# Rotating 96 images: all stores moved from SyncE to GpSimd, each transfer asked for as one packet per engine

## The chip, the cores and the metric

The kernel runs on one core of one Trainium2 chip. The metric is the device time of that core in microseconds (us); lower is better. One execution was also taken by the hardware profiler, and all views below are of that one.

## The reference

The input is 32 x 3 = 96 images of 256 x 256 float32 values. Each is turned by 90 degrees clockwise.

```python
def reference(x: np.ndarray) -> np.ndarray:
    return np.rot90(x, k=-1, axes=(-2, -1)).astype(np.float32)
```

There is no arithmetic in it. 25.17 MB are read from device memory (HBM) and 25.17 MB are written to it.

## The kernel before

The 96 images are cut into 12 slabs (`n_slabs`) of 8 images, 2.097 MB each. A slab stands in on-chip memory (SBUF) as 128 partitions with 4096 values, in two halves (`I = 2`). There are two ways to lay its rows over the partitions: "short", where a partition holds a run of 8 rows from each half (two pieces of 8 KB per partition), and "long", where a run of 16 rows lies together (one piece of 16 KB, and a half occupies 64 partitions). All twelve slabs fit in SBUF at once; `units` holds them. Slabs 3 and 7, 8 and 9, and 10 and 11 lie next to each other in one tile each (`pairs`).

The work has three stages.

- **Loads.** The loop at line 86 issues all loads on SyncE's queue (SP), slab after slab. Slabs 0, 1 and 2 use the short layout, the others the long one in two halves of 1.049 MB. The first half of the last slab is cut in two (lines 94 to 96), and its larger part, 896 KB, is kept as `mark` (line 98). After it come only the other 128 KB of that half and the slab's second half.
- **Turns.** `turn(n)` (line 102) moves a slab with VectorE's 32 x 32 transposes (line 118), in 2 instructions, or in 4 for two slabs at once in the pairs from 8 and 10 on. Each turn writes into the place of a slab that has been turned before (`home`); the first goes to PSUM (`turned0`). The turn of slab 8 writes over slabs 3 and 7's tile, so it has to wait until the store that reads that tile (`store(4)`, the first) has read it.
- **Stores.** `store(n)` (line 120) issues the stores of a slab, also on SP. The five slabs 4, 3, 5, 6 and 7 go in one transfer of 2.097 MB with 8 KB pieces (line 132). Slabs 1, 2 and 0 go in two transfers of 1.049 MB with 16 KB pieces (line 130). The pairs 8/9 and 10/11 go in one transfer of 2.097 MB (line 124) and two of 1.049 MB (line 127), all with 16 KB pieces. That makes 17 stores.

The order of the stores is written by hand at line 136, and the first of them is made to wait until `mark` has landed (line 139). After that, SP issues them in program order, each when its data are turned. A queue also goes through eight completion semaphores in turn, so a transfer waits for the one eight places before it.

At the end ScalarE copies slab 0 from PSUM to SBUF in two instructions (line 146), and the last two stores write it out.

Of the kernel before, what the change touches and what calls it, by code (L numbers as in the profile page):

```python
# [1 line left out]

# [4 lines left out]

@with_exitstack
def kernel(
    ctx: ExitStack,
    tc: tile.TileContext,
    x: bass.AP,
    out: bass.AP,
):

    nc = tc.nc
    fp32 = mybir.dt.float32

    B, C, H, W = x.shape
    P = nc.NUM_PARTITIONS
    RL, RS = 16, 8  # L50
    I = 2
    Q = P * RS // H
    n_slabs = B * C // (Q * I)
    last = n_slabs - 1
    F = RS * W
    long_st = (0, 1, 2)
    both = (8, 10)
    paired = [n + a for n in both for a in range(2)]

    rows_in = x.rearrange("b c h w -> (b c h) w")  # L60
    rows_out = out.rearrange("b c h w -> (b c h) w")

    def short(rows):
        return rows.rearrange("(n i p r) w -> n p i (r w)", i=I, p=P, r=RS)

    def long(rows):
        return rows.rearrange("(n i m r) w -> n i m (r w)", i=I, m=P // I, r=RL)

    ld_short, ld_long, st_short, st_long = short(rows_in), long(rows_in), short(rows_out), long(rows_out)

    units = [None] * n_slabs
    adjacent = [(3, 7), (8, 9), (10, 11)]
    pairs = []
    for us in adjacent + [(u,) for u in range(n_slabs) if all(u not in us for us in adjacent)]:
        pool = ctx.enter_context(tc.tile_pool(name=f"unit{us[0]}", bufs=1))
        held = pool.tile([P, len(us), I * F], fp32, name=f"u{us[0]}")
        for j, u in enumerate(us):
            units[u] = held[:, j]
        pairs.append(held)
    psum = ctx.enter_context(tc.tile_pool(name="psum", bufs=1, space=bass.MemoryType.PSUM))  # L80
    turned0 = psum.tile([P, I * F], fp32, name="turned0")

    def fours(t):
        return t.rearrange("p (i f) -> p i f", i=I)

    for n in (0, 1, 2, 3, 7, 4, 5, 6, *range(8, n_slabs)):
        if n in (1, 2):
            nc.sync.dma_start(out=fours(units[n]), in_=ld_short[n])
            continue
        for i in range(I):  # L90
            if n in long_st:
                ld = nc.sync.dma_start(out=fours(units[n])[:, i], in_=ld_short[n][:, i])  # L92
            else:
                cuts = (0, 14 * W, RL * W) if (n, i) == (last, 0) else (0, RL * W)
                for f0, f1 in zip(cuts, cuts[1:]):
                    ld = nc.sync.dma_start(out=units[n][i::I, f0:f1], in_=ld_long[n, i][:, f0:f1])
                    if f1 == 14 * W:
                        mark = ld

    home = [turned0] + units[:last]  # L100

    def turn(n):
        if n in long_st:
            src = fours(units[n]).rearrange("p i (r g c) -> p c r g i", r=RS, c=RL)
            dst = home[n].rearrange("p (c k r) -> p c r k", c=RL, r=RS)[:, :, ::-1, ::-1]
            parts, step = 2, RL // 2
        elif n in paired:
            if n not in both:
                return
            src = pairs[both.index(n) + 1].rearrange("p a (r g c) -> p c r g a", r=RL, c=RL)  # L110
            dst = pairs[both.index(n)].rearrange("p i (c k r) -> p c r k i", c=RL, r=RL)[:, :, ::-1, ::-1, :]
            parts, step = 4, RL // 4
        else:
            src = units[n].rearrange("p (r g c) -> p c r g", r=RL, c=RS)
            dst = fours(home[n]).rearrange("p i (c k r) -> p c r k i", c=RS, r=RL)[:, :, ::-1, ::-1, :]
            parts, step = 2, RS // 2
        for h in range(parts):
            nc.vector.transpose(out=dst[:, h * step : (h + 1) * step], in_=src[:, h * step : (h + 1) * step])  # L118

    def store(n):  # L120
        if n in paired:
            first = n if n in both else n - 1
            if n == first:
                nc.sync.dma_start(out=st_long[n].transpose([1, 0, 2]), in_=pairs[both.index(n)][::I])
                return
            for i in range(I):
                nc.sync.dma_start(out=st_long[n, i], in_=pairs[both.index(first)][n - first :: I, i])
        elif n in long_st:
            for i in range(I):
                nc.sync.dma_start(out=st_long[n, i], in_=home[n][i::I])  # L130
        else:
            return nc.sync.dma_start(out=st_short[n], in_=fours(home[n]))

    for n in range(both[0]):
        turn(n)
    for n in (4, 3, 5, 6, 7, 1, 2):
        st = store(n)
        if n == 4:
            tc.add_manual_dep(st.ins, mark.ins.name, mybir.DependencyInfo(
                mybir.DependencyClass.Sync, mybir.DependencyReason.SCHED_ONLY), reason="stores after loads")  # L140
    for n in range(both[0], n_slabs):
        turn(n)
        store(n)

    for i in range(I):
        nc.scalar.copy(out=fours(units[last])[:, i], in_=fours(turned0)[:, i])  # L146
    home[0] = units[last]
    store(0)


# [1 line left out]
_INS = ['x']  # L152
_OUTS = [((32, 3, 256, 256), 'float32')]


# [23 lines left out]
```

## Time and profile before

| what | value |
|---|---|
| three timed runs | 123.1, 123.28, 123.25 us (median 123.25) |
| span of the profiled execution, first to last instruction | 121.4 us |
| what lies around it | the profiled execution's own time is not listed apart; the median of the runs is 1.85 us above the span |
| VectorE busy | 90.5 us in 24 transposes |
| ScalarE busy | 4.9 us (one table load, two copies) |
| GpSimd busy | 0.2 us (four memsets) |
| DMA | 4800 packets, 50.33 MB, all on one queue; 98.0% of the 16 engines' time |
| loads issued on SP | 23, from 0.73 to 45.5 us |
| stores issued on SP | 17, from 59.46 to 105.4 us |

How to read it: the page divides the span into 40 equal slices, and shows for each the busy share of an engine in tenths and what the DMA engines moved. A stretch line gives the same for a time window. Issuing a transfer is not counted as busy time of the engine that issues it; those instructions are found under "SPq" for SyncE's queue and "POOLq" for GpSimd's. A packet in the DMA count is a piece of data of 2, 8 or 16 KB, or one of the 16 small writes that report the completion of a transfer.

### The profile page before, as it was taken

The numbers are of one execution on the slowest core, as the hardware profiler recorded it, in microseconds if no ns is written. First come the engines' busy times: TensorE is split into PE (matmuls) and PEld (weight loads), VectorE is DVE, ScalarE is ACT, GpSimd is POOL, SyncE is SP. The second block draws the span as 40 slices with busy tenths as digits, with TensorE's granted clock in tenths as the row PEclk, the third lists the DMA queues.
The fourth block names the chain that finished last, engine by engine and source line by source line (L and its number), as shares of the span: only waits on it lengthen the run. The fifth ranks groups of instructions, "written<-read, shape, count | busy, mean of one in ns | idle before, by whom it ended". The sixth has DMA issues, their size and how long they took to land.

```text
span 121.4 us, 134 instructions
## 1 busy us (share of the span) xinstructions
DVE 90.5 (75%) x24; ACT 4.9 (4%) x3; POOL 0.2 (0%) x4
## 2 busy tenths in 40 slices
DVE  0029999999999999999999999999999960000000
ACT  0000000000000000000040000000000038000000
POOL 0000000000000000000000000000000000000000
DMA  3999999999999999999999999999999999999994
GB/s 84 416 432 424 426 459 432 432 432 426 426 432 426 416 421 432 421 426 450 403 424 426 426 429 429 421 432 424 464 426 432 432 432 432 432 432 432 432 432 178
DMA packets 4800, 50.33 MB, mean 414 GB/s; under 512 B 640, under 2 KB 640, under 8 KB 704
## 3 DMA queue, kind: packets, MB, share of 16 engines
q1 hardware_dynamic: 4800, 50.33, 98.0%
HBM read 25.17 MB, written 25.17 MB: 414 GB/s over the span
## 4 chain that ended last, share of the span: by engine, by line
DVE 55%; issue 17%; DMA 6%; DVEq 3%; ACT 2%; ACTq 1%; SPq 0%
DVE u L118 50%; DVE turned L118 6%; DMA u<-in_x_dram 6%; DVEq L174 3%; ACT u L146 2%; ACTq L174 1%; SPq L92 0%; DVEq L118 0%
## 5 line engine op out<-in xcount | busy, mean ns | idle before, releaser
L118 DVE STREAM_TRANSPOSE u<-u 128x2048 f32<-128x2048 f32 x22 | 83.4, 3861 | 0.3
L118 DVE STREAM_TRANSPOSE turned<-u 128x2048 f32<-128x2048 f32 x2 | 7.1, 3584 | 8.3 <-DMA u<-in_x_dram 8.3
L146 ACT COPY u<-turned 128x2048 f32<-128x2048 f32 x2 | 3.6, 1869 | 35.6 <-DVE u L118 35.6
L146 ACT ACT_TABLE_LOAD x1 | 1.3, 1283 | 62.3 <-DMA u<-in_x_dram 62.3
L163 POOL MEMSET const-uint8-127<- 128x1 uint8 x1 | 0.1, 103 | 0.0
L163 POOL MEMSET const-bfloat16-1.0<- 128x1 bf16 x1 | 0.1, 101 | 0.0
L163 POOL MEMSET const-float32-0.0<- 128x1 f32 x1 | 0.1, 99 | 0.2 <-issue 0.2
L163 POOL MEMSET const-float32-1.0<- 128x1 f32 x1 | 0.1, 99 | 0.0
## 6 DMA issues: line engine op xcount, KB each, us to landing
u<-in_x_dram SPq DMA_DIRECT2D x19, 1024.0 KB, 19.6
out_dram<-u SPq DMA_DIRECT2D x7, 2048.0 KB, 16.3
out_dram<-u SPq DMA_DIRECT2D x10, 1024.0 KB, 18.3
u<-in_x_dram SPq DMA_DIRECT2D x2, 2048.0 KB, 13.7
u<-in_x_dram SPq DMA_DIRECT2D x1, 896.0 KB, 19.3
u<-in_x_dram SPq DMA_DIRECT2D x1, 128.0 KB, 17.2
```

Of the source, the lines that this page charges most:

```text
L118: nc.vector.transpose(out=dst[:, h * step : (h + 1) * step], in_=src[:, h * step : (h + 1) * step])
L146: nc.scalar.copy(out=fours(units[last])[:, i], in_=fours(turned0)[:, i])
L163: nc = _bacc.Bacc("TRN2", target_bir_lowering=False, num_devices=1)
L174: with _tile.TileContext(nc) as tc:
```

## The change

Every store is issued by GpSimd instead of SyncE, through a new helper `put`, with `single_packet=True`. This asks for all pieces that one DMA engine handles in a transfer to be one packet. The stores keep their shapes and their order: `follow` chains each to the one before it in GpSimd's program. The first store still waits for `mark`. The loads, the turns and the copies stay as they are. The stores now go through eight completion semaphores of their own.

```diff
+    def put(out, in_):
+        follow(nc.gpsimd.dma_start(out=out, in_=in_, single_packet=True))
+
     def store(n):
         if n in paired:
             first = n if n in both else n - 1
             if n == first:
-                nc.sync.dma_start(out=st_long[n].transpose([1, 0, 2]), in_=pairs[both.index(n)][::I])
+                put(out=st_long[n].transpose([1, 0, 2]), in_=pairs[both.index(n)][::I])
                 return
             for i in range(I):
-                nc.sync.dma_start(out=st_long[n, i], in_=pairs[both.index(first)][n - first :: I, i])
+                put(out=st_long[n, i], in_=pairs[both.index(first)][n - first :: I, i])
         elif n in long_st:
             for i in range(I):
-                nc.sync.dma_start(out=st_long[n, i], in_=home[n][i::I])
+                put(out=st_long[n, i], in_=home[n][i::I])
         else:
-            return nc.sync.dma_start(out=st_short[n], in_=fours(home[n]))
+            put(out=st_short[n], in_=fours(home[n]))
...
+    behind = [mark]
+
+    def follow(st):
+        first = behind[0] is mark
+        tc.add_manual_dep(st.ins, behind[0].ins.name, mybir.DependencyInfo(
+            mybir.DependencyClass.Sync if first else mybir.DependencyClass.NoSync,
+            mybir.DependencyReason.SCHED_ONLY), reason="order of the stores")
+        behind[0] = st
+
     for n in (4, 3, 5, 6, 7, 1, 2):
-        st = store(n)
-        if n == 4:
-            tc.add_manual_dep(st.ins, mark.ins.name, mybir.DependencyInfo(
-                mybir.DependencyClass.Sync, mybir.DependencyReason.SCHED_ONLY), reason="stores after loads")
+        store(n)
```

## The prediction

> **What bounds the kernel now.** I began with the page's slices, because a kernel that only moves and turns data should show its limit there.
>
> ```profile
> span 121.4 us, 134 instructions
> DVE 90.5 (75%) x24; ACT 4.9 (4%) x3; POOL 0.2 (0%) x4
> DMA  3999999999999999999999999999999999999994
> GB/s 84 416 432 424 426 459 432 432 432 426 426 432 426 416 421 432 421 426 450 403 424 426 426 429 429 421 432 424 464 426 432 432 432 432 432 432 432 432 432 178
> q1 hardware_dynamic: 4800, 50.33, 98.0%
> ```
>
> Every slice but the first and last has the DMA engines at 9 tenths or more, at about 430 GB/s, and one queue carries all 50.33 MB. The chain of waits does name VectorE for 55%, but that chain is followed through waits; the transfers that run full beside it are the limit. VectorE stops at 99.08 us and data moves for 20 us more. So the sum is: start, 50.33 MB at a rate, end. Next I read stretches (us from:to, then busy time of VectorE, ScalarE and GpSimd, TensorE clock, DMA share, GB/s).
>
> ```profile
> 2.40:2.80 0.40, 0.00 (x0) 0.00 (x0) 0.00 (x0) 1.00 0.51 164
> 2.80:3.20 0.40, 0.00 (x0) 0.00 (x0) 0.00 (x0) 1.00 0.94 389
> 60.00:63.00 3.00, 2.97 (x2) 0.74 (x1) 0.00 (x0) 1.00 0.97 412
> 63.00:86.00 23.00, 22.93 (x7) 0.55 (x1) 0.00 (x0) 1.00 1.02 431
> 88.00:118.00 30.00, 11.07 (x4) 3.63 (x2) 0.00 (x0) 1.00 1.00 429
> 119.40:119.80 0.40, 0.00 (x0) 0.00 (x0) 0.00 (x0) 1.00 0.86 369
> 119.80:120.20 0.40, 0.00 (x0) 0.00 (x0) 0.00 (x0) 1.00 0.02 0
> ```
>
> Data flows from 2.8 us, turns from loads to stores around 61 to 62 us with hardly a dip (412 against 430 for 3 us: 3 x 18/430 = 0.13 us lost), and stops at 119.8, 1.6 us before the span ends. Last I read the store issues and what stands at the ends (ns min/median/max, first and last start).
>
> ```profile
> L132 SPq DMA_DIRECT2D out_dram<-u x5: 372/389/947, 59.5 to 70.2; - x5
> L124 SPq DMA_DIRECT2D out_dram<-u x2: 626/636/647, 84.7 to 99.1; - x2
> L127 SPq DMA_DIRECT2D out_dram<-u x4: 1367/1381/1397, 85.3 to 101.2; - x4
> L130 SPq DMA_DIRECT2D out_dram<-u x6: 1242/1346/1381, 70.6 to 104.0; - x6
> L146 ACT ACT_TABLE_LOAD x1 | 1.3, 1283 | 62.3 <-DMA u<-in_x_dram 62.3
> L174 POOLq DRAIN  x3: 34/41/70, 0.7 to 121.2; - x3
> ```
>
> The first store is issued at 59.46 us, when the marked load has landed; the last near 104 us. For the spread of the rate I took stretches of 10 us:
>
> ```profile
> 10.00:20.00 10.00, 9.96 (x4) 0.00 (x0) 0.00 (x0) 1.00 1.04 439
> 50.00:60.00 10.00, 9.96 (x4) 0.00 (x0) 0.00 (x0) 1.00 1.00 421
> 90.00:100.00 10.00, 9.07 (x3) 0.90 (x1) 0.00 (x0) 1.00 1.02 437
> ```
>
> **The change, part by part.** The time starts from the span of 121.4 us. The profiled execution's own time is not listed apart from that; the three runs have a median of 123.25, 1.85 us more, and I carry this 1.85 unchanged. Bytes, transfers and the order of the stores stay.
>
> *17 issues leave SP.* 5 x 0.389 + 2 x 0.636 + 4 x 1.381 + 6 x 1.346 = 16.8 us of SP's time. It is worth nothing: SP has issued its last load by 45.5 us and only stores came behind, and the transfers were full while SP issued them. The loads keep their times to 59.46.
>
> *17 issues arrive at GpSimd*, which had done four memsets by 0.43 us and is idle after. Their cost there is not in the trace. A 2 MB store takes 2.097 MB / 0.430 = 4.88 us to move and a 1 MB store 2.44 us, so an issue hurts a running stream only above 2.44 us per 1 MB, 1.75 times the longest SP row (1.397). Bounds: 0.37 to 1.4 us each, hidden at both ends. Behind each waiting store on GpSimd's queue stand only later stores, as on SP. The stores of the slabs 8 and 10 wait for VectorE (84.66 and 99.10 us); ahead of slab 10's lie 6 x 2.097 + 6 x 1.049 = 18.9 MB of stores, which last from 62.2 to 62.2 + 18.9/0.430 = 106.1 us. So that store has 7 us in hand and needs 2 to 4.
>
> *The turn from loads to stores* is where the first store's delay can show. When it is released, 128 KB and 1 MB of loads (1.18 MB) are still to move: 2.74 us, to 62.2; ScalarE's table load, which waits for them, starts at 62.26. That is the cover. What SP's path needs: first load issued at 0.73, rate built up between 1.6 and 2.8, so 0.9 to 2.1 us. What GpSimd adds is not shown. Low end: 0.9 + 0.37 = 1.3 us, covered, and a separate queue may even win the 0.13 us of the dip. High end: 2.1 + 1.4, and 1.28 for a first use as the table load on ScalarE costs, 4.8 us, a hole of 2.1 us. I take 0.4, nearer the covered end, because the middle of the issue rows (about 0.9) on the middle start (1.5) makes 2.4, inside the cover, and 0.4 is a fifth of the high end for a path that no row shows. Who waits for the first store: VectorE's slab 8 overwrites its source. A store landed 7.6 us after issue at the earliest, which fits this one: 67.1; VectorE came to it at 70.4: 3.3 us to spare, and the 3 us of slab 10's store behind that. Cost nothing.
>
> *One packet per engine.* A 2 MB store becomes 2.097 MB/16 = 131 KB per engine, 4.88 us without a break, where the packets of before were 8 or 16 KB (4800 packets). Two consequences. If engines alternate between the load and the store queue, the last loads, at most 1.4 us = 0.6 MB of them when stores begin (under three 16 KB pieces per engine), wait for up to three such packets, 14.6 us, and land near 77 instead of 62.3. Their reader is VectorE's slab 10 at 88.35: hidden, with room for two packets more. The other is the rate. The 8 KB rows (63 to 86 us) ran at 431, the 16 KB rows (88 to 118) at 429: twice as many pieces cost nothing that can be seen, so fewer packets have little to win, 0.5% of 58.5 us = 0.3 us. By the spread of 10 us stretches in the trace (421 to 439, and 437 in the stores) the outer bounds are 58.5 x (1 - 430/437) = 0.94 won and 58.5 x (430/421 - 1) = 1.25 lost. I take 0, the equality of the two rows being the nearest evidence. The Trainium skill, DMA: Bandwidth & Descriptors, "Why small descriptors are slow (HBM only)", states a fixed overhead of about 3 cycles per packet inside the DMA engine, against 32 bytes per cycle, which by estimate is 1.2% at 8 KB and 0.6% at 16 KB and would let this change win 0.29 + 0.20 = 0.5 us (122.75). It asks for a slower stretch with 8 KB rows, and this trace has a faster one, 431 against 429.
>
> *The end.* Completion of 17 transfers is now settled on GpSimd, whose three drains took 34 to 70 ns with nothing behind them. Bounds: 0, and 17 x 0.07 = 1.2 us if each transfer costs a drain; below nothing by no more than the 0.1 of SP's part. I take 0.2, since most transfers are done long before.
>
> Sum: 0.4 + 0 + 0.2 = +0.6, span 122.0, time 123.85. This case's own range is 123.2 to 125.2 (hole 0 to 1.5, end 0 to 0.5).
>
> **The rivals.** *Faster: the stream itself gains.* The pieces' breaks vanish and the stores start beside the loads: 0.94 + 0.13 at most, 122.2; with half of it 122.7. For it: the rate swings between 421 and 439, so 430 may not be the ceiling. Against: 431 with 8 KB rows.
>
> *Slower: VectorE shuts GpSimd out.* VectorE runs from 8.25 to 99.08 us with breaks of some 0.02 us. If GpSimd can prepare a store only between two transposes, the first waits from 59.46 to 62.4, when the transpose in progress ends, then needs 2.4 (the middle above) to 3.5 us (2.1 + 1.4): 64.8 to 65.9, a hole of 2.6 to 3.7 us, time 123.25 + 2.6 + 0.2 = 126.0 to 127.1. Later stores stay hidden, as one transpose (3.86 us) is shorter than one 2 MB store. It decides from a wait of over 0.3 us, what the cover of 2.74 leaves over 2.4. Nothing in this trace has GpSimd and VectorE at work together. The Trainium skill, SBUF — State Buffer, "Who interferes with whom", speaks against the change: a VectorE instruction in a two-port mode locks GpSimd out of the SBUF port that it writes descriptors with. It lists copies, casts and tensor_scalar and not the transpose: the rule makes the hole of this rival if the transpose belongs to them, and nothing if not, and no row here shows which.
>
> *Slower: a pause between packets.* If an engine ends each big packet before it begins the next, the pause is about the start's 0.9 us, 17 times: 15.3 us, 138. It decides at the second store. Against it: before, whole transfers followed each other with no gap.
>
> *No change*: the packet request has no effect and the turn is covered: 123.25.
>
> **How the numbers follow.** My forecast case has 0.48, of which 0.05 lies within 0.2%; faster stream 0.27; no change 0.10; shut out 0.09; pauses 0.06. What a measurement can tell from no change is 0.2%, 0.25 us (three runs spread over 0.18). So faster 0.27, within 0.15, slower 0.58. The range 122.4 to 127.1 leaves out the pauses, the best ends of the faster case and the longest holes, under 0.2 in all.
>
> **What would show it.** After: a second queue with 25.17 MB, and fewer packets there than 2448 (1280 of 8 KB, 896 of 16 KB and 17 x 16 for completion, the stores' part of the 4800); loads with unchanged times; the first bytes of stores, which I expect 2.5 to 3.5 us after the mark; stores at 428 to 432 GB/s (a rate of 435 or more is the faster rival, a comb of holes the pauses); VectorE still done by about 99 to 101; at most 2 us between the last byte and the end. If VectorE's transposes grow or the first store begins only at a transpose's end, the lock is at work. I am wrong if the stores' rate moves by over 1%.

## The result and the profile after

The changed kernel takes 126.11 us (125.93 to 126.14 in 4 runs) against 123.20 us for the kernel before (the median of four runs here): a ratio of 1.0235, with a 95% interval of 1.022 to 1.0249. It is 2.9 us slower. The prediction had the sign and, with its range of 122.4 to 127.1, the time, but its most likely value was 123.85: it saw 0.6 us of 2.9.

The page after, in the lines that answer to those shown of before:

```profile
span 124.3 us, 144 instructions
DVE 90.6 (73%) x24; ACT 4.9 (4%) x3; POOL 10.6 (9%) x21
DMA  4999999999999999999999999999999999999991
GB/s 84 427 424 422 435 448 443 432 422 427 422 422 422 422 432 427 427 437 430 355 387 422 424 422 408 424 427 430 424 427 422 422 422 406 401 432 432 427 427 47
q0 software_dynamic: 2448, 25.17, 48.9%
q1 hardware_dynamic: 2352, 25.17, 48.4%
```

VectorE and ScalarE do what they did. The stores are now on a queue of their own (q0), with exactly the 2448 packets that the stores had before. Two marks are new in the row of GB/s: 355 and 387 at the turn from loads to stores (slices 20 and 21), and dips to about 401 to 408 behind some later slices in which GpSimd is busy. The same in stretches of the changed kernel (us from:to, then busy time of VectorE, ScalarE, GpSimd, TensorE clock, DMA share, GB/s):

```profile
59.00:64.00 5.00, 4.97 (x2) 1.28 (x1) 3.00 (x4) 1.00 1.00 369
70.00:76.00 6.00, 5.97 (x3) 0.00 (x0) 2.92 (x5) 1.00 1.00 412
106.00:112.00 6.00, 0.00 (x0) 0.00 (x0) 0.00 (x0) 1.00 0.97 412
```

and in those of the kernel before:

```profile
59.00:64.00 5.00, 4.97 (x2) 1.28 (x1) 0.00 (x0) 1.00 0.99 420
70.00:76.00 6.00, 5.97 (x3) 0.00 (x0) 0.00 (x0) 1.00 1.02 431
106.00:112.00 6.00, 0.00 (x0) 0.00 (x0) 0.00 (x0) 1.00 1.01 431
```

The DMA share stays near 1 in both (0.97 to 1.02): the engines are hardly idle, their pieces take longer. (The last of these stretches overstates it: its pieces take 616 ns on average for 611.) The last view is the end of the changed kernel, and its stores (ns min/median/max, first and last start):

```profile
L121 POOL DMA_DIRECT2D out_dram<-u x17: 547/560/843, 60.0 to 103.6; - x17
L183 SPq DRAIN  x3: 7/7/7, 123.0 to 123.8; - x3
L183 POOLq DRAIN  x3: 34/101/20062, 103.5 to 124.1; - x3
```

GpSimd's drain begins at 103.5, lasts 20.06 us and ends at 123.6, 0.6 us after SyncE stands at its own drain (123.0). The barrier that ends the kernel waits for it.

Stretches swing by some 10 GB/s with where their edges cut a piece, so for the accounting I used two records of the trace behind these views: the duration of every single piece, and the time at which each of the 16 engines reports the completion of each transfer. Taking the 16th report each time (the semaphore that the program waits for moves 0.3 to 0.5 us later, for the first store before at 67.08 us):

| | before | after | difference |
|---|---|---|---|
| first store landed | 66.60 | 67.67 | +1.07 |
| from there to the last store's landing | 53.67 | 54.83 | +1.16 |
| from the last piece's end to the end of the span | 1.16 | 1.83 | +0.67 |
| sum | | | +2.90 |

The whole loss is in this table. In the kernel before every 8 KB store piece takes 309 ns and every 16 KB piece 611, within 4%. In the changed kernel eleven of the first pieces take 639 to 1578 ns, those between 72 and 76 us 322 on average (up to 432), and the 16 KB pieces from 86 to 90 and from 100 to 106 us 642 to 645 (up to 774). These are the 2 to 4 us that follow GpSimd's groups of issues at 60, 70.5, 85 and 99 us. Between them pieces are almost back at 309 and 611. The slow pieces don't fall on all engines alike: the reports of a transfer come within 0.45 us before, and after the change they end in two groups of eight that together spread over 1.29 us. These two things make up the first two rows: all store pieces together lose 1.70 us per engine, and the last report comes 0.68 us after the mean of the sixteen instead of 0.23, so 1.70 + 0.45 = 2.15 of the 2.23 us.

### The profile page after: what moved, and what is told of

It reads as the page before. It is cut to its first block, busy times and chain, and to the rows that moved or that the text cites. A ratio compares the mean times of both kernels' runs of the same rounds, so it can differ in the third digit from the quotient of the medians.

```text
span 124.3 us, 144 instructions
## 1 busy us (share of the span) xinstructions
DVE 90.6 (73%) x24; ACT 4.9 (4%) x3; POOL 10.6 (9%) x21
## 3 DMA queue, kind: packets, MB, share of 16 engines
q0 software_dynamic: 2448, 25.17, 48.9%
## 4 chain that ended last, share of the span: by engine, by line
DMA 65%; issue 13%; SPq 2%; DVE 2%; POOL 2%; POOLq 0%; DVEq 0%
DMA u<-in_x_dram 45%; DMA out_dram<-u 19%; DVE u L118 2%; POOL out_dram L121 2%; SPq L88 1%; SPq L92 1%; POOLq L183 0%; SPq L96 0%; DVEq L118 0%; POOLq L121 0%
## 5 line engine op out<-in xcount | busy, mean ns | idle before, releaser
L118 DVE STREAM_TRANSPOSE u<-u 128x2048 f32<-128x2048 f32 x22 | 83.5, 3872 | 0.3
L121 POOL DMA_DIRECT2D out_dram<-u x17 | 10.4, 617 | 93.2 <-DMA u<-in_x_dram 59.5
```

The costliest lines, as they stand in the source:

```text
L121: follow(nc.gpsimd.dma_start(out=out, in_=in_, single_packet=True))
```

## The experiments

My theory after this comparison was that GpSimd's path costs all three terms and that the packet request costs nothing. The rivals were the large packet, a second queue of any kind, and VectorE keeping GpSimd away. Below, "excess" is the time of store pieces over 309 or 612 ns (those more than some 4 to 5% over), summed and divided by 16 engines; it is 1.28 us in the changed kernel (1.70 with all pieces, as above) and 0 before. Every ratio is to the kernel before, run on the same chip.

**1. The change without the packet request.**

```diff
-        follow(nc.gpsimd.dma_start(out=out, in_=in_, single_packet=True))
+        follow(nc.gpsimd.dma_start(out=out, in_=in_))
```

> Theory: the 2.9 us that the change costs come from the path through GpSimd (cold first pieces 0.65 us, pieces slowed after each group of issues 1.1 us, the remainder at the end), and the packet request has no part in it: without it 126.1, within 0.3. Rival: the request for one large packet slows the pieces: without it the rate is back at 430 GB/s and the time near 125.0; if it also makes the cold start, 124.3.

Measured: 126.12 us, ratio 1.0232 (1.0215 to 1.0249), span 124.3 as in the change, excess 1.32 us. The request has no part in the loss.

**2. The packet request alone, on SyncE.** In the kernel before, every store gets the request.

```diff
-                nc.sync.dma_start(out=st_long[n, i], in_=home[n][i::I])
+                nc.sync.dma_start(single_packet=True, out=st_long[n, i], in_=home[n][i::I])
...
```

> Stores stay on SyncE behind the loads, with the request for one packet alone. Theory: the request costs nothing that is seen: 123.2, within 0.3, pieces of 309 and 612 ns as before. Rival (the large packet is what slows): 124.3 or more.

Measured: 123.23 us, ratio 0.9997 (0.9989 to 1.0006), no piece over its 309 or 612 ns by 5%. On SyncE the request changes nothing that can be measured either. Its half of the change is empty at these transfers.

**3. All stores on ScalarE's queue.**

```diff
-        follow(nc.gpsimd.dma_start(out=out, in_=in_, single_packet=True))
+        follow(nc.scalar.dma_start(out=out, in_=in_))
```

> All stores on ScalarE's queue, no packet request: a second queue beside the loads, as with GpSimd, but not GpSimd's path. Theory: only the cold start of an unused queue remains, 123.2 + 0.65 = 123.9 (123.5 to 124.2), stores at 430 GB/s, end as before. Rival: any second queue costs the slowed pieces and the end as well: 126.1.

Measured: 123.25 us, ratio 1.0000 (0.9991 to 1.0009). I had expected 0.65 us for an unused queue, and there is nothing: 431 GB/s through the turn, excess 0.01 us, and 1.16 us from the last piece to the end as before. A second queue is free; GpSimd's is not.

```profile
59.00:64.00 5.00, 4.97 (x2) 0.00 (x0) 0.00 (x0) 1.00 1.02 431
70.00:76.00 6.00, 5.97 (x3) 0.00 (x0) 0.00 (x0) 1.00 1.02 431
```

**4. GpSimd's queue used once at the start.**

```diff
+    warm = ctx.enter_context(tc.tile_pool(name="warm", bufs=1)).tile([P, 128], fp32, name="warm")
+    nc.gpsimd.dma_start(out=warm, in_=rows_in[:P, :128], single_packet=True)
```

> The changed kernel with one more load of 64 KB (128 partitions x 512 bytes, its data unused) issued by GpSimd at the start. Theory: the slow first pieces belong to the first use of a queue in the kernel; with that spent in the load stage the stretch from 59 to 64 us is back at 415 to 420 GB/s, time 126.1 - 0.65 + 0.15 for the added bytes = 125.6. Rival: they belong to every start of an idle queue: 126.1 to 126.3.

Measured: 126.19 us, ratio 1.0235 (1.0217 to 1.0252). No piece of a store that starts before 62 us takes over 316 ns, where eleven took 639 to 1578, and the stretch from 59 to 64 us is at 428 GB/s, above the 415 to 420 that the theory asked. The time stays. The first store lands at 67.28 us instead of 67.67, but from there to the last landing it takes 55.35 us for 54.83, and the last store lands at 122.63 for 122.51; the added load itself makes up some 0.2 us of that (experiment 10: 0.17). Pieces between 62 and 66 us take 328 ns on average for 317, and those between 72 and 76 us 336 for 322; the second group varies from run to run, as it took 333 in experiment 1 too. So first use explains the very slow first pieces, and without them the stream lost later what the first store won. My reading fell here.

**5. The last five stores back on SyncE.**

```diff
+        eng, kw = (nc.sync, {}) if hw[0] else (nc.gpsimd, dict(single_packet=True))
+        follow(eng.dma_start(out=out, in_=in_, **kw))
...
+        hw[0] = n >= both[1]
         store(n)
```

(`hw[0]` is set for slab 0 too.)

> The changed kernel with its last five stores (slabs 10, 11 and 0, 6.3 MB) back on SyncE. Theory: the end costs 0.65 us more only because GpSimd's closing drain outlasts the last transfer on GpSimd's queue, and the group of issues near 100 us slows pieces; with GpSimd done some 5 us before the end both go: 126.1 - 0.65 - 0.3 = 125.1 (124.9 to 125.4), last landing to end of span back at 1.1 us. Rival: the end belongs to a kernel that has used GpSimd's queue at all: 125.8 to 126.1.

Measured: 125.29 us, ratio 1.0172 (1.0158 to 1.0186), last piece to end 1.46 us instead of 1.83. The time is as expected, the split is not: in the profile, 0.37 us come from the end and 0.50 from the stream (last landing 122.00). The end is still 0.30 us longer than in the kernel before, although GpSimd's drain was over at 85.9 + 26.6 = 112.5 us, so this part is not the drain's.

**6. The first two stores on SyncE as well.** To the edit before, `hw[0] = n in (4, 3)` is added in the loop of the first stores, and GpSimd's first store (slab 5) waits for the mark too.

> As the one before, and the first two stores (slabs 4 and 3, 4.2 MB) on SyncE too, GpSimd's first store (slab 5) waiting for the same marked load: GpSimd has 10 stores in the middle, 14.7 MB less 0.0 for what moved, beside SyncE's. Theory: the slow first pieces of GpSimd's queue lie beside SyncE's stores, which go on: 125.1 - 0.6 to - 1.0 = 124.1 to 124.5, and what is left over 123.2 are the pieces slowed after GpSimd's issues. Rival (as the added early load suggested, what is won at the first store is lost in later slowing): 125.0 or more.

Measured: 123.70 us, ratio 1.0045 (1.0032 to 1.0057), below the expected 124.1 to 124.5. Two transfers moved bring 1.6 us. GpSimd issues 10 stores, all but the first at the same times as in the change, VectorE runs beside them, and no 8 KB piece of its queue takes over 325 ns; excess 0.13 us. Nearly all of that lies from 86 to 90 us, where the 16 KB pieces take 632 ns on average for 642 in the change: the group of issues at 85 us still slows them, with SyncE's queue empty since 77.5 us. GpSimd's first store, issued at 60.04 us, also has more time here, as its first piece starts only at 65.21, behind SyncE's.

**7 and 8. Smaller pieces, on GpSimd and on SyncE.** The ten 1 MB stores go in 4 KB pieces.

```diff
+        cut = dict(max_dma_last_dim=4096) if len(out.shape) == 2 else {}
+        follow(nc.gpsimd.dma_start(out=out, in_=in_, single_packet=True, **cut))
```

> The changed kernel with the ten 1 MB stores cut into pieces of 4 KB instead of 16 KB, same transfers, same number of issues: 2560 pieces for 640. Theory: what slows the running pieces is the preparing and reading of GpSimd's piece lists, so it grows with the number of pieces: the bursts after 70, 85 and 99 us, which hold eight of the ten, slow two to three times as much, 127.2 to 129. Rival: the cost is by issue: 126.1 to 126.4.

> The control: the kernel of before, all on SyncE, with the same ten stores in pieces of 4 KB. Theory: SyncE's path has no price by piece that is seen at these sizes: 123.2 to 123.5. Rival: small pieces are slower on any path, 1% or more of the 24.4 us that these stores take to move: 123.5 to 124.

Measured: GpSimd 127.75 us, ratio 1.0372 (1.0357 to 1.0386); SyncE 124.17, ratio 1.0081 (1.0068 to 1.0095). The first alone would have looked like a hit for the theory. The control takes 0.98 us of its 1.64 away: a piece has a price on SyncE too, 0.98 us for (2560 - 640)/16 = 120 pieces more per engine, about 8 ns each. The rest, 0.66 us, is GpSimd's: from the first store's landing to the last, experiment 7 takes 1.84 us more than its control (56.51 against 54.67), where the change takes 1.16 more than the kernel before. So the slowing grows with the pieces (4096 for 2176, and four times as many in ten of the transfers), but in less than proportion.

**9. Every second store on SyncE.** Within `put`, even stores go to SyncE and odd ones to GpSimd, the first of these after the mark.

> The 17 stores in the same order, every second one on SyncE (first and last among them, 9 in all), the other 8 on GpSimd as in the change. Theory, as the run with both ends on SyncE suggests: pieces of GpSimd's queue are slow only while an engine has that queue alone to work from; with SyncE's queue filled beside it nearly none is, 123.2 to 123.5 (0.2 us or so of that at the end). Rival: the cost goes with what GpSimd prepares, half of the pieces and half of the 2.9 us: 124.4 to 124.9.

Measured: 123.51 us, ratio 1.0024 (1.0015 to 1.0034), excess 0.05 us, last piece to end 1.21 us. GpSimd prepares 8 transfers, and the pieces hardly slow. This is the theory's upper end, and the rival (half the loss) is out. But GpSimd's first store, issued at 60.07 us, has its first piece at 65.22 here too, so this run and the sixth don't tell SyncE's work beside the queue from a store that is issued well ahead.

**10. The kernel before with the small early load on GpSimd.** The two added lines of experiment 4, on the kernel before.

> The kernel of before with one load of 64 KB on GpSimd's queue at the start, its data unused, all stores on SyncE. Theory: a GpSimd queue that has long been empty costs nothing at the end but 0.15 to 0.25 us for the load's bytes: 123.3 to 123.5, and landing to end of span 1.1 us. Rival: some 0.2 to 0.6 us at the end belong to having used the queue at all: 123.6 to 124.0.

Measured: 123.60 us, ratio 1.0031 (1.0020 to 1.0041), at the lower edge of the rival's range. The last landing is 0.17 us later, as the load's bytes ask, and the end takes 1.34 us for 1.16. Experiment 2's profile took 1.30 us there without GpSimd's queue, so this is no more than a bound: to have used that queue early costs at most some 0.2 us at the end.

**11. An earlier release of the first store.** The mark is slab 10's last load.

```diff
-                    if f1 == 14 * W:
+                    if (n, i) == (10, 1):
                         mark = ld
```

> The changed kernel, its first store waiting for slab 10's last load instead of slab 11's larger piece, so that 2.1 MB of loads (4.9 us) are still to come instead of 1.2 MB. Theory: the first pieces of GpSimd's queue are slow beside loads that fill the engines, and the hole of about 1 us at the first store goes: 125.0 to 125.5. Rival (as the added early load showed): what is won there is lost again while GpSimd's queue is alone: 125.8 to 126.1.

Measured: 124.48 us, ratio 1.0105 (1.0091 to 1.0119), better than the theory's 125.0. All 17 stores are on GpSimd, and the first is issued at 57.86 instead of 59.98. Its first piece starts at 61.36, hardly earlier than the 61.43 of the change, but at full speed. All pieces up to 86 us take at most 322 ns, although GpSimd issues its groups at 70.5 and 85 us as before and has the engines to itself. What slows is the last group, at 99 us.

```profile
59.00:64.00 5.00, 4.97 (x2) 1.28 (x1) 1.85 (x3) 1.00 1.00 424
70.00:76.00 6.00, 5.97 (x3) 0.00 (x0) 2.91 (x5) 1.00 1.01 429
106.00:112.00 6.00, 0.00 (x0) 0.00 (x0) 0.00 (x0) 1.00 0.97 412
L183 POOLq DRAIN  x3: 34/93/18333, 103.6 to 122.4; - x3
```

The last store lands at 120.82 (before 120.27), and the drain ends at 103.6 + 18.3 = 121.9, 1.1 us after it, as in the change (123.6 against 122.5). Of the 1.2 us that are left, the end has 0.67 and the stream from the first to the last landing 0.61.

**12. More issues, the same pieces.** The five 2 MB stores go out as ten of 1 MB.

```diff
-            put(out=st_short[n], in_=fours(home[n]))
+            for i in range(I):
+                put(out=st_short[n][:, i], in_=fours(home[n])[:, i])
```

> The changed kernel with its five 2 MB stores of 8 KB pieces issued as ten of 1 MB: 22 issues for 17, the same pieces. Theory: the cost is not by issue: 126.1 to 126.3. Rival: each issue costs its share of the slowed pieces, 1.16/17 = 0.07 us, and more at the drain: 126.5 or more.

Measured: 126.24 us, ratio 1.0248 (1.0234 to 1.0262), with the last landing as in the change (122.57 for 122.51) and 2.02 us for the end (1.83 in the change). The stream has no price by issue.

**13. A release in between.** Slab 11's first half is cut at `7 * W` instead of `14 * W`.

> The changed kernel with slab 11's first half cut after 7 of 16 rows instead of 14, so that the first store is released about 1.1 us earlier (near 58.4 us, between the change's 59.5 and the earlier release's 57.4), all else as in the change. If the lead of GpSimd's first store over the end of the loads decides both the hole and the later slowing: the hole shrinks to 0 to 0.4 us and the time lies between 124.5 and 125.4. If only a much earlier start helps: 125.8 to 126.1.

Measured: 124.91 us, ratio 1.0136 (1.0123 to 1.0149). The first store is issued at 58.91 and lands at 66.56, no later than before (66.60): the hole is gone with an issue 1.07 us earlier, as expected if the lead decides. Slowing is almost absent at 72 to 76 us (0.02 us of the excess, against 0.15 in the change), and sets in with the group at 85 us. With an issue 2.1 us earlier (experiment 11) it sets in at 99 us.

**14. The earlier release, and the last five stores on SyncE.** The edits of 11 and 5 together.

> The earlier release (slab 10's last load) with the last five stores on SyncE: GpSimd still issues 12 stores, and has the engines alone from 62 to 99 us. Theory, that a GpSimd queue with its pieces prepared ahead runs at the full rate: no slowed piece until 99 us, end at 1.3 us after the last landing, 123.2 + 0.1 to 0.4 = 123.3 to 123.6. Rival, that GpSimd's issues slow pieces wherever its queue is alone: 124.2 or more.

Measured: 123.72 us, ratio 1.0035 (1.0023 to 1.0047), a tenth above the theory's range and far from the rival. GpSimd issues 12 stores, and from 62 to 99 us the engines work from its queue alone; excess 0.05 us. The last store lands at 120.56, and the end takes 1.46 us as in experiment 5, for an expected 1.3; GpSimd's drain is over at 109.2 us.

```profile
59.00:64.00 5.00, 4.96 (x2) 1.28 (x1) 1.86 (x3) 1.00 0.99 417
70.00:76.00 6.00, 5.97 (x3) 0.00 (x0) 2.91 (x5) 1.00 1.01 427
82.00:88.00 6.00, 5.97 (x2) 0.00 (x0) 1.71 (x3) 1.00 1.06 449
```

GpSimd is busy in all three stretches (2.91 us in five issues in the second), as it was in the change, and the rate holds. A group of issues by itself doesn't slow the pieces.

Put together, the three terms of the loss by the lead of GpSimd's first store (from its issue to the end of the loads' last piece, 61.7 us in each):

| | lead | first store landed | first to last landing | end | excess | first group with slow pieces | time |
|---|---|---|---|---|---|---|---|
| the kernel before | | 66.60 | 53.67 | 1.16 | 0 | none | 123.20 |
| the change | 1.7 us | 67.67 | 54.83 | 1.83 | 1.28 us | 60 us | 126.11 |
| experiment 13 | 2.8 us | 66.56 | 54.68 | 1.86 | 0.39 us | 85 us | 124.91 |
| experiment 11 | 3.8 us | 66.54 | 54.28 | 1.83 | 0.22 us | 99 us | 124.48 |
| 14: as 11, last five stores on SyncE | 3.8 us | 66.56 | 54.00 | 1.46 | 0.05 us | none of weight | 123.72 |

The excess is a mean over 16 engines and leaves out pieces that are little over; the stream loses more than that, since the slower eight engines set its end.

**What stays open.** Shown is that GpSimd's queue takes over at full rate when its first store is issued 2.8 to 3.8 us before the loads end instead of 1.7, and that the groups of issues that follow then slow the pieces less and later: with 3.8 us it was the group at 99 us alone that did so with weight. The end doesn't change with the lead. With SyncE's stores in front (experiments 6 and 9) the stream is nearly whole as well, but there the first store is also issued 5.2 us before its first piece, so no run shows what SyncE's work beside the queue does by itself. Why a late start is still felt 10 to 25 us later, although the queue then holds whole transfers in hand, why the slow pieces gather on eight of the engines, and where the 0.30 us at the end come from that stay when GpSimd's drain is long over, no run here shows.

## Why the prediction was right or wrong

**The bound.** Right: the transfers bound both kernels. The DMA share stays at 9 tenths in every inner slice, and the loads run as before (428 GB/s from 4 to 59 us in both).

**SP relieved, GpSimd loaded.** Right: 17 issues fewer on SP gain nothing; an issue on GpSimd takes 547 to 843 ns, inside the 0.37 to 1.4 us that the SP rows gave, and is hidden. Experiment 12 has five more and no later landing.

**The turn, 0.4 taken, 1.07 measured.** The place was right, the mechanism only in part, and the size wrong. The first piece does start inside the cover, at 61.43, 1.9 us after the mark has landed and about when the loads run out (in the kernel before the first piece of a store starts at 61.26), so the path to the first byte cost little. But the first pieces are slow: I added up a path to the first byte, 2.4 us, where the stream at full rate is what counts. And the cover was shorter than my 2.74 us: the marked load's pieces had ended at 58.9 us, those of the next 128 KB at 59.2, when its landing released the store at 59.5, so less than 1 MB was left, up to 61.7: 2.1 us. Experiment 13, released at 58.46, 3.2 us before the loads' end, loses nothing at the turn. My high end of 2.1 held the value. The 0.4 was not worked out of a row at all.

**The rate, 0 taken, 1.16 lost.** This is the step that failed most: the stores take 54.83 us from the first landing to the last for 53.67, 2.2% more. I asked whether larger packets change the rate and took the equality of two stretches, 431 and 429, for an answer; I had no term for what GpSimd's queue does to pieces that already run, and gave the whole uncertainty to the packets. The outer bound of 1.25 held it by its width, not by its reason. And the two stretches were misread: by single pieces, 16 KB take 611 ns and two of 8 KB 618, 1% more, and the control with 4 KB pieces paid 0.98 us. So a piece does have a price, of some 7 to 8 ns.

The Trainium skill, DMA: Bandwidth & Descriptors, "Why small descriptors are slow (HBM only)", which I had set behind the stretches, is on the side of these pieces: by its about 3 cycles, two pieces of 8 KB would take 0.6% longer than one of 16 KB (an estimate: 518 cycles for 515). Measured are 618 ns for 611, 1.1%, so a piece costs here about twice what the page gives. What it would have let the change win, 0.5 us, didn't come, as the request leaves 2448 packets as 2448 and 309 ns as 309 (experiments 1 and 2).

**The large packets between the loads.** The waiting that I described, a load piece behind 131 KB of stores, did not occur: ScalarE's table load, which waits for the last load, starts at 62.23, and at 62.26 before.

**The end, 0.2 taken, 0.67 measured.** The bounds of 0 and 1.2 were right, the choice wrong: "most transfers are done long before" is no reason, since GpSimd's drain waits for the last one and ends 1.07 us after its landing, where SyncE needs less than 0.5. With GpSimd's drain long over, 0.30 of the 0.67 us are still there (experiments 5 and 14), so at most 0.37 of them are the drain's. (By single pieces the data of before stop at 120.27 us, 1.16 before the end, and not at 119.8.)

**VectorE.** Right: slab 8's turn and all the rest end as before (99.08 us in both), with the first store landing 1.07 us later.

**The rivals.** VectorE shutting GpSimd out was priced at 126.0 to 127.1, and 126.11 lies in it, but not for its reason. The first store is issued 0.45 us after its release and in the middle of a transpose, and a transpose takes 3,872 ns for 3,861. The same group of three stores takes GpSimd as long beside transposes, at 84.94, as behind the last of them, at 99.38 (start and duration in us, what ran, and in brackets the idle time before and what ended it):

```profile
84.94 1.72 POOL L121 DMA_DIRECT2D out_dram<-u  x3 [11.53 <-DVE u L118]
99.38 1.72 POOL L121 DMA_DIRECT2D out_dram<-u  x3 [12.72 <-DVE u L118]
```

Pieces slow as well between 100 and 106 us, where VectorE is idle, and experiments 6, 9 and 14 keep VectorE and lose nearly all the slowing. The range reached up to 126.11 by this rival alone, as the forecast case ended at 125.2; that it holds the time is luck. The Trainium skill, SBUF — State Buffer, "Who interferes with whom", does not name the transpose among the instructions that lock GpSimd out, and no lock shows in these runs. A pause between packets didn't occur. The faster stream didn't either. "No change" was right about the request and wrong about the queue.

**What would have shown it.** The list named the first bytes (2.5 to 3.5 us after the mark; they came after 1.9), the rate (428 to 432; the pieces after each group ran up to 6% slower on average, and all stores together 2.2%, more than the 1% that I had named as the sign of being wrong) and the end (at most 2 us after the last byte; 1.83).

## What to carry to other kernels

Two kernels with the same transfers can differ by the queue that asks for them: here ScalarE's was free and GpSimd's cost 2.9 us, most of which came back when its first store was released 2.1 us earlier and the last stores went to SyncE. When a stream passes from one queue to another, ask how early the new queue must be told to be at full rate at once, not when its first byte moves, and which engine's drain the end of the kernel then waits for. And run the control: a hit of 1.6 us for smaller pieces on GpSimd was 1.0 us of something that SyncE pays too.

## What the hardware showed that I had not expected

- A queue on ScalarE that had not been used before took over the stream at 431 GB/s with no loss at all, although the same handover to GpSimd lost 1.07 us.
- A warm-up of GpSimd's queue (experiment 4) removed pieces of 0.6 to 1.6 us and gained nothing; a lead of one more microsecond gained 1.2 us.
- Sixteen engines that share a stream evenly came apart in two groups of eight, 1.29 us from the first to the last of their reports on the last transfer, and the slower group set the time.
- A store that was issued 3.8 us before the loads' end did not move beside them: its first piece started at 61.36 us, when the loads' pieces ran out, in spite of a queue of its own.
